# Latent attention: probabilities as the stationary operand, the result divided with queries on partitions and turned by TensorE

## The chip, the cores and the metric

The kernel runs on one core of one Trainium2 chip. A core has TensorE (matmuls), VectorE, ScalarE, GpSimd and SyncE, which run side by side and wait for each other through semaphores; DMA engines move data between the chip's memory (HBM) and the on-chip SBUF. TensorE writes into PSUM. In the profile the engines are called PE (TensorE's matmuls), PEld (its weight loads, that is loads of the stationary operand), DVE (VectorE), ACT (ScalarE), POOL (GpSimd) and SP (SyncE). The metric is the device time of one execution in microseconds. The kernel before takes 2379.64 us (median of 3 runs, 2379.31 to 2381.75).

## The reference

Two layers on 1024 tokens of width 1024, in float32. Layer 0 mixes tokens by differential attention, layer 1 by latent attention; each is followed by a gated MLP with a causal convolution, and a norm closes the whole. The change is in the latent attention of layer 1 alone. Cut to that:

```python
def mla_attention(h, w_in, q_norm_g, kv_norm_g, w_uq, w_ukv, w_o, cos, sin):
    ...                                   # q_nope, q_pe, k_nope, k_pe, v from latents; 16 heads
    scale = (MLA_NOPE + MLA_ROPE) ** -0.5         # (64 + 32) ** -0.5
    def block(args):                              # one block of 128 queries
        qn, qp, blk = args
        sc = (jnp.einsum('bqhd,bkhd->bhqk', qn, k_nope)
              + jnp.einsum('bqhr,bkr->bhqk', qp, k_pe)).astype(jnp.float32) * scale
        p = masked_softmax(sc, chunk_mask(blk, s)[None, None])
        return jnp.einsum('bhqk,bkhe->bqhe', p.astype(v.dtype), v)   # v has 64 columns per head
    ...
    return o.reshape(b, s, MLA_HEADS * MLA_V) @ w_o
```

The mask lets a query see the keys of its own chunk of 64 tokens and of all chunks before it. So query block i (128 queries) needs i + 1 key blocks of 128.

## The kernel before

Numbers are split into a high and a low part of a reduced float format (fp32r); a product of two split numbers takes three matmuls (`mm3`, lines 119 to 121), each with a stationary and a moving operand. `hi` (line 127, a cast, mostly on ACT) makes the high part and `lo` (line 130, a subtraction on DVE or POOL) the low one.

The latent attention works in 64 steps, 16 heads of 4 (`MlaStep`, line 1981; `attend`, line 1781). Step p of a head treats query blocks 2p and 2p + 1, so 256 queries. The order of p is 1, 0, 3, 2, and 3, 2, 1, 0 in the last head. A step does:

- `scores(j)` for its two query blocks j: queries stationary, keys moving, 3 matmuls per 512 keys, into PSUM "S" (two buffers of 1024 columns); a memset for the mask (line 1999), the row maximum (line 2000), then exp with the sum l of each row (line 2001). Queries are on partitions.
- `weigh(j)` (line 2005): a reciprocal of l on DVE (line 2007) and a multiplication of all probabilities of the block by it on POOL (`scale`, line 149).
- `turn` (line 254): 128x128 blocks of probabilities are transposed by TensorE (line 263, four or three into one bank of PSUM "b") and split by `hi` and `lo` into `pt[g]`, keys on partitions. A full group holds in this order: first key block for query block 0, the same for query block 1, second key block for 0, for 1. The last group leaves out what the mask hides and holds three blocks.
- `product` (line 2010): for each key block of 128, V is stationary (128 keys on partitions; 64 columns of its high part and 64 of its low part side by side) and the transposed probabilities are moving, low part and then high part, 256 queries wide, or 128 for the last key block. The result in PSUM "u" (one buffer) has V's columns on partitions: 64 for the high part of V, 64 for the low. ACT copies one half and DVE adds the other (lines 2024, 2025) into a tile `o` of 64x512 for each head and half of the tokens, and when its two steps are done a DMA on ACT's queue writes it to `o_d` in HBM (line 2027). `finish` does nothing.

`steps` (line 292) writes the work of neighbouring steps interleaved: step t's scores and the key and query projections of the next pair of heads (`units`, `q_unit`, `k_unit`), step t - 1's transposes between the two scores, and its product after the second; `finish` is called for step t - 2. The projections of the last pair are done before its steps start, so its steps have none beside them. Within a layer's attention here no order is written out by hand (there is one for the other attention, `manual_schedule`); the order of instructions on each engine is chosen when the program is built, by a planner that runs its own simulation with its own costs (`schedule_with_timeline_sim`, line 2314), from the dependences and the written order. On the chip each engine then works in that fixed order.

Beside the attention POOL and DVE split weights and values of the next pair (`split_w`, `split_v`), and, in the last 10 steps, the output projection's weights are fetched and split. The output projection reads `o_d` back, 128 tokens at a time and four pairs of heads at once (`project_load`, line 659), with the columns of two heads on 128 partitions.

Of the kernel before, what the change touches and what calls it, by code (L numbers as in the profile page):

```python
# [17 lines left out]

P = 128
S = 1024  # L20
D = 1024
NT = S // P
KD = D // P
EPS = 1e-6
# [12 lines left out]
FFN = 2816  # L37
NF = FFN // P


def blocks(n, step=512):
    return [(a, min(step, n - a)) for a in range(0, n, step)]


class Ring:


    def __init__(self, k, *places):
        self.k, self.places, self.n = k, places, 0
# [7 lines left out]
class Trunk:  # L57
# [7 lines left out]
    def __init__(self, tc, ctx, a):  # L65
# [226 lines left out]
    def steps(self, attend, units, prepare, n, apart=False):  # L292


        steps = []
        for t in range(n + 2):
            now = before = None
            u = []
            if t < n:
                now = attend(t)  # L300
                steps.append(now)
                prepare(t)
                u = units(t)
                now.scores(0)
            if 0 < t <= n:
                before = steps[t - 1]
            alone = u[:-1] if apart else []
            if alone:
                u = u[-1:]
            self.run(alone or u, 2 if alone else 1)  # L310
            if before:
                before.turn()
            self.run(alone)
            if now:
                now.weigh(0)
                now.scores(1)
            self.run(u)
            if before:
                before.product()
            if now:  # L320
                now.weigh(1)
            if t >= 2:
                steps[t - 2].finish()
            yield
# [1331 lines left out]
    def mla_heads(self, cT, v_d, o_d):  # L1656
        nc, a = self.nc, self.a
        pairs = MLA_HEADS // 2
        heads = [dict() for _ in range(MLA_HEADS)]
# [4 lines left out]
        cs = self.at("u13", [P, S])  # L1664
        nc.sync.dma_start(cs, a["rope_q"])
        R = SimpleNamespace(
            P=self.ring("u12", "u6", "u7", "u8", "u9"), pT=self.ring("u0", "u1", "u10", "u11"), o=self.ring("h4", "h5", "h6", "h7"),
        )

        eng = lambda x: {"S": None, "V": nc.vector, "P": nc.gpsimd}[x]  # L1670
# [129 lines left out]
class Step:  # L1800


    def __init__(self, k, R, h, p, heads):
        self.k, self.R, self.h, self.p, self.hd, self.heads = k, R, h, p, heads[h], heads
        self.l, self.probs = [], []

    def turn(self):
        self.pt = self.k.turn(self.R.pT, self.p, self.probs)
# [2 lines left out]
class DaStep(Step):  # L1811
# [37 lines left out]
    def scores(self, j):  # L1849
        k, nc, hd = self.k, self.k.nc, self.hd  # L1850
        i = 2 * self.p + j
        n = (i + 1) * P
        q = hd["q"][i // 4]
        qs = slice((i % 4) * P, (i % 4 + 1) * P)
        sc = self.sc[j] = []
        for c in range(2):
            if c == 0 or not self.one:
                ps = k.big()
            sc.append(ps[:, c * 512 : c * 512 + n] if self.one else ps[:, :n])
        self.both[j] = ps.rearrange("p (c n) -> p c n", c=2)  # L1860
# [65 lines left out]
    def product(self, g):  # L1926
        k, p = self.k, self.p
        if self.o is None:
            self.o = k.bank()[:, :256]
        for kb, (ah, al), c0 in k.key_blocks(p, {x: self.pt.get(x, self.pt[g]) for x in range(p + 1)}):  # L1930
            if kb // 2 == g:
                vh, vl = (self.hd["v"][kb // 4][:, part, (kb % 4) * P : (kb % 4 + 1) * P] for part in range(2))
                k.mm3(self.o[:, c0:], vh, vl, ah, al, kb == 0, kb == 2 * p + 1)
# [47 lines left out]
class MlaStep(Step):  # L1981
    def __init__(self, k, R, h, p, heads, V, o_d):
        super().__init__(k, R, h, p, heads)
        self.V = V
        self.dst = o_d[h // 2, (h % 2) * 64 : (h % 2) * 64 + 64, (p // 2) * 512 : (p // 2 + 1) * 512]

    def scores(self, j):
        k, nc = self.k, self.k.nc
        i = 2 * self.p + j
        n = (i + 1) * P  # L1990
        q, kt = self.hd["q"], self.hd["k"]
        qs = slice(i * P, (i + 1) * P)
        nm, l = k.stat(), k.stat()
        if j == 0 or n > 512:
            self.e = self.R.P([P, S])
        sc, e = k.big()[:, :n], self.e[:, :n] if n > 512 else self.e[:, j * 512 : j * 512 + n]
        for b, m in blocks(n):
            k.mm3(sc[:, b : b + m], q[:, 0, qs], q[:, 1, qs], kt[:, 0, b : b + m], kt[:, 1, b : b + m], True, True)
        nc.vector.memset(sc[0:64, n - 64 : n], NEG)
        nc.vector.tensor_reduce(nm, sc, axis=AX.X, op=ALU.max, negate=True)  # L2000
        nc.scalar.activation(e, sc, AF.Exp, bias=nm, accum_out=l)
        self.l.append(l)
        self.probs.append(e)

    def weigh(self, j):
        nc, l, e = self.k.nc, self.l[j], self.probs[j]
        nc.vector.reciprocal(l, l)  # L2007
        self.k.scale(e, l[:, 0:1], "P")

    def product(self):  # L2010
        k, nc, h, p = self.k, self.k.nc, self.h, self.p
        cols = slice((p % 2) * 256, (p % 2 + 1) * 256)
        half = p // 2
        first = ("o", half) not in self.hd
        if first:
            self.hd["o", half] = self.R.o([64, 512])
        t = self.hd["o", half]
        o = k.bank("u")[:, :256]
        for kb, (ah, al), c0 in k.key_blocks(p, self.pt):
            v = self.V[h // 2][:, kb, h % 2].rearrange("p a e -> p (a e)")  # L2020
            nc.tensor.matmul(o[:, c0:], v, al, start=kb == 0, stop=False)  # L2021
            nc.tensor.matmul(o[:, c0:], v, ah, start=False, stop=kb == 2 * p + 1)  # L2022

        nc.scalar.copy(t[:, cols], o[64:128])
        nc.vector.tensor_add(t[:, cols], t[:, cols], o[0:64])
        if not first:
            nc.scalar.dma_start(self.dst, t)

    def finish(self):
        pass  # L2030


def kernel_body(tc, a, out):
    with ExitStack() as ctx:
# [144 lines left out]
        heads = k.mla_input(W_in, hts, turns, v_d, lambda cT: k.mla_heads(cT, v_d, o_d[1]))  # L2179
        W = []  # L2180
        step, finish, rest = prefetcher(a["mla_w_o"], W, slots(2, 3, 6, 7, 1, 10, 0, 11), units(6, 7, 8, 9))
        heads.rest(step)
        finish()
        places = iter(units(2, 3, 4, 5, 12, 13, 10, 11))
        X = k.project_first(W, o_d[1], k.ring(*halves(0, 1, 2, 3)), x_d[1], lambda q, i: k.at(next(places), [P, D]), 0, rest)
# [132 lines left out]
```

## Time and profile before

The profiled execution took 2379.93 us, of which the span from the first to the last instruction is 2378.1 us.

| | |
|---|---|
| median of 3 runs | 2379.64 us |
| profiled execution, its span | 2379.93 us, 2378.1 us |
| mean granted TensorE clock | 0.999 |
| busy: PE, PEld, DVE, ACT, POOL | 2346.4, 1975.7, 1925.3, 1246.5, 587.5 us |
| first and last product of the latent attention | 1312 us and 1650 us after the span's start |
| matmuls of the product (lines 2021 and 2022) | 640, of them 512 with 256 columns and 128 with 128 |
| transposes of the probabilities (line 263) | 576 |
| reciprocals (line 2007), copies and additions of the result (lines 2024, 2025) | 128, 64 and 64 |
| DMA writes of the result (line 2027) | 32 of 128 KB |

How to read it: "busy" is the union of an engine's records, and TensorE's records are as long as a matmul takes from entering to leaving the array, so that neighbours overlap; what a matmul costs a busy TensorE is the distance to the start of the next. A group's row gives line, engine, operation, what is written and read, the shapes, the count, then busy time, mean length in ns, and the idle time of the engine before it with what ended it. A row of waits gives who waited for whom, the total in us, how often, and, where there is a third number, the longest.

### The profile page before, as it was taken

The page shows a single profiled execution, that of the slowest core. Times are in us where ns is not written, and L with a number is a line of the kernel's source. Part 1 is how long each engine was busy: PE and PEld are TensorE (multiplying, and loading weights), DVE is VectorE, ACT ScalarE, POOL GpSimd, SP SyncE. Part 2 cuts the span into 40 slices and gives each one's busy share as a digit, 9 for nine tenths or more (in the row PEclk, how much of TensorE's full clock was granted, in tenths as well). Part 3 has the DMA queues.
Part 4 walks back from the last instruction along what each step waited for, and adds up shares of the span by engine and source line. Part 5 has one row for each costly group of instructions (what it writes and reads, how often), then busy time and mean ns, then how long its engine had stood idle before and what let it go on. Part 6 is the DMA issues. An engine that isn't in the chain of part 4 may idle for free.

```text
span 2378.1 us, 32958 instructions
## 1 busy us (share of the span) xinstructions
PE 2346.4 (99%) x12146; PEld 1975.7 (83%) x12146; DVE 1925.3 (81%) x3170; ACT 1246.5 (52%) x2301; POOL 587.5 (25%) x465
## 2 busy tenths in 40 slices
PE   9999999999999999999999999999999999999998
PEld 7888888788888888888898889988788888888886
DVE  6777877859888888999855888886588888889997
ACT  5666666745444444354444778775354444443544
POOL 4545444324000000000133666673420000000001
PEclk9999999999999999999999999999999999999999
DMA  3111111342222222652221211133322222227502
GB/s 148 40 36 36 49 37 54 114 130 86 93 84 80 80 88 81 233 176 84 84 98 56 72 33 39 41 98 114 108 72 94 82 80 80 89 80 283 177 1 80
DMA packets 95667, 213.42 MB, mean 90 GB/s; under 512 B 8713, under 2 KB 33937, under 8 KB 95505
## 3 DMA queue, kind: packets, MB, share of 16 engines
q1 hardware_dynamic: 86304, 183.51, 23.6%
q10 hardware_dynamic: 9200, 27.80, 3.2%
q8 instruction: 96, 1.57, 0.3%
q14 instruction: 67, 0.54, 0.1%
HBM read 158.85 MB, written 52.43 MB: 89 GB/s over the span
## 4 chain that ended last, share of the span: by engine, by line
PE 89%; DVE 5%; DMA 2%; ACT 2%; issue 1%; POOL 0%; POOLq 0%; DVEq 0%; ACTq 0%; SPq 0%
PE S L119 13%; PE S L121 13%; PE S L120 13%; PE b L119 9%; PE b L120 8%; PE b L121 8%; PE u L119 5%; PE u L121 4%; PE u L120 4%; PE S L1866 3%; PE b L263 2%; PE u L2022 1%; PE u L2021 1%; PE b L1912 1%; DVE s L130 1%
## 5 line engine op out<-in xcount | busy, mean ns | idle before, releaser
L167 POOL TENSOR_TENSOR st<-st,mhalf 128x1 f32<-128x1 f32 x56 | 35.4, 633 | 1301.5 <-DVE st L164 1291.4
L121 PE MATMUL S<-s,u 128*128 128x512 f32 (+1 forms) x800 | 301.3, 377 | 1.1 <-POOL u L130 1.0
L119 PE MATMUL S<-s,u 128*128 128x512 f32 (+1 forms) x800 | 301.8, 377 | 0.2 <-ACT u L1092 0.2
L120 PE MATMUL S<-s,u 128*128 128x512 f32 (+1 forms) x800 | 301.0, 376 | 0.0
L127 ACT CAST u<-h 128x512 fp32r<-128x512 f32 (+1 forms) x194 | 115.8, 619 | 274.4 <-DVE h L1013 262.2
L119 PE MATMUL b<-s,u 128*128 128x512 f32 x588 | 230.8, 393 | 1.1 <-DVE u L130 0.4
L120 PE MATMUL b<-s,u 128*128 128x512 f32 x588 | 229.0, 389 | 0.0
L121 PE MATMUL b<-s,u 128*128 128x512 f32 x588 | 229.0, 389 | 0.0
L1070 DVE SCALAR_TENSOR_TENSOR u<-u,conv,u 128x1023 f32<-128x1023 f32 (+1 forms) x176 | 225.0, 1278 | 0.8 <-ACT u L1066 0.7
L149 POOL TENSOR_TENSOR u<-u,st 128x512 f32<-128x512 f32 (+7 forms) x160 | 173.2, 1091 | 161.4 <-DVE st L2007 107.5
L127 ACT CAST s<-u 128x512 fp32r<-128x512 f32 (+3 forms) x229 | 144.0, 663 | 97.8 <-PE u L121 28.3
L127 ACT CAST u<-b 128x512 fp32r<-128x512 f32 (+1 forms) x256 | 134.8, 547 | 92.1 <-PE b L1912 57.7
L130 DVE TENSOR_TENSOR u<-b,u 128x512 fp32r<-128x512 f32 (+1 forms) x256 | 158.5, 631 | 23.7 <-ACT u L127 22.6
L121 PEld LDWEIGHTS S<-s,u 128*128 128x128 f32 x800 | 150.5, 188 | 29.2 <-POOL u L130 1.4
L119 PEld LDWEIGHTS S<-s,u 128*128 128x128 f32 x800 | 150.5, 188 | 27.9 <-ACT u L1092 0.5
L120 PEld LDWEIGHTS S<-s,u 128*128 128x128 f32 x800 | 150.6, 188 | 27.2
L119 PE MATMUL u<-s,s 128*128 128x512 f32 (+1 forms) x408 | 165.2, 405 | 1.1 <-DVE s L130 0.9
L121 PE MATMUL u<-s,s 128*128 128x512 f32 (+1 forms) x408 | 158.3, 388 | 0.0
L120 PE MATMUL u<-s,s 128*128 128x512 f32 (+1 forms) x408 | 157.6, 386 | 0.0
L130 DVE TENSOR_TENSOR s<-u,s 128x512 fp32r<-128x512 f32 (+2 forms) x205 | 140.7, 720 | 16.4 <-ACT s L127 15.9
L1073 ACT ACTIVATE u<-u 128x1024 f32<-128x1024 f32 x44 | 46.7, 1062 | 187.6 <-DVE u L1070 187.6
L130 DVE TENSOR_TENSOR u<-h,u 128x512 fp32r<-128x512 f32 x171 | 117.9, 689 | 32.4 <-ACT u L127 31.5
(290 smaller groups left out, 6384.9 us busy)
## 6 DMA issues: line engine op xcount, KB each, us to landing
u<-in_ffn_up SPq DMA_DIRECT2D x88, 512.0 KB, 4.2
g_d<-u ACTq DMA_DIRECT2D x44, 512.0 KB, 2.6
u<-in_ffn_down SPq DMA_DIRECT2D x66, 256.0 KB, 4.9
u<-g_d SPq DMA_DIRECT2D x62, 256.0 KB, 3.9
s<-in_da_wqkv SPq DMA_DIRECT2D x23, 512.0 KB, 3.3
x_d<-u SPq DMA_DIRECT2D x16, 512.0 KB, 3.0
s<-x_d SPq DMA_DIRECT2D x8, 1024.0 KB, 10.8
s<-g_d SPq DMA_DIRECT2D x18, 256.0 KB, 5.3
```

The source lines that it names most:

```text
L119: mm(out, lh, rl, start=first, stop=False, skip_group_check=onto)
L120: mm(out, lh, rh, start=False, stop=False, skip_group_check=onto)
L121: mm(out, ll, rh, start=False, stop=last, skip_group_check=onto)
L127: self.nc.scalar.copy(out, src)
L130: (eng or self.nc.vector).tensor_sub(out, src, hi.bitcast(F32))
L149: self.nc.gpsimd.tensor_mul(x, x, s.to_broadcast(list(x.shape)))
L167: nc.gpsimd.tensor_tensor(r, s, self.mhalf, ALU.pow)
L263: self.nc.tensor.transpose(ps[:, j * P : (j + 1) * P], probs[t][:, k : k + P], self.ident)
L1070: nc.vector.scalar_tensor_tensor(t[half][:, back:], u[half][:, : S - back], w, t[half][:, back:], ALU.mult, ALU.add)
L1073: nc.scalar.activation(t[0], t[0], AF.Silu)
L1866: nc.tensor.matmul(sc[c][:, b : b + m], q[rows, qp, qs], kt[rows, kp, :m], start=x == 0, stop=x == 2)
L1912: k.nc.tensor.transpose(ps[:, j * P : (j + 1) * P], self.e[t][0][:, c : c + P], k.ident)
```

## The change

The product's operands change places. For each of the two query blocks and each key block that it may see, the transposed probabilities (128 keys x 128 queries; low part, then high part) are stationary and V (128 keys x 128 columns, high and low part side by side) is moving. The result has queries on partitions, in PSUM "u": for each query block 64 columns for the high and 64 for the low part of V.

The probabilities are no longer scaled: `weigh` goes. Both row sums of a step stand in one tile of two columns, one reciprocal inverts both, and after ACT's copy of the low half and DVE's addition of the high half, POOL multiplies the 128x128 result by the inverse row sums. The results of the two heads of a pair stand side by side in one tile of 128 queries x 4 query blocks x 128 columns for each half of the tokens. `finish` of every step with odd head and even p turns this tile: four transposes by TensorE into one bank of "b", a copy by ACT, and one DMA of 128x512 to `o_d` from ACT's queue. The layout of `o_d` stays.

```diff
@@ steps @@
             self.run(alone)
             if now:
-                now.weigh(0)
                 now.scores(1)
             self.run(u)
             if before:
                 before.product()
-            if now:
-                now.weigh(1)
             if t >= 2:
                 steps[t - 2].finish()
...
@@ mla_heads @@
-            P=self.ring("u12", "u6", "u7", "u8", "u9"), pT=self.ring("u0", "u1", "u10", "u11"), o=self.ring("h4", "h5", "h6", "h7"),
+            P=self.ring("u12", "u6", "u7", "u8", "u9"), pT=self.ring("u0", "u1", "u10", "u11"), o=self.ring("h4", "h5", "h6", "h7"), oT=self.ring("h12", "h13"),
...
@@ MlaStep @@
-        self.dst = o_d[h // 2, (h % 2) * 64 : (h % 2) * 64 + 64, (p // 2) * 512 : (p // 2 + 1) * 512]
+        self.dst = o_d[h // 2, :, (p // 2) * 512 : (p // 2 + 1) * 512]
+        self.pair = heads[h - h % 2]
+        self.l = k.stat(2)
...
-    def weigh(self, j):
-        nc, l, e = self.k.nc, self.l[j], self.probs[j]
-        nc.vector.reciprocal(l, l)
-        self.k.scale(e, l[:, 0:1], "P")
 
     def product(self):
...
-        for kb, (ah, al), c0 in k.key_blocks(p, self.pt):
-            v = self.V[h // 2][:, kb, h % 2].rearrange("p a e -> p (a e)")
-            nc.tensor.matmul(o[:, c0:], v, al, start=kb == 0, stop=False)
-            nc.tensor.matmul(o[:, c0:], v, ah, start=False, stop=kb == 2 * p + 1)
-
-        nc.scalar.copy(t[:, cols], o[64:128])
-        nc.vector.tensor_add(t[:, cols], t[:, cols], o[0:64])
-        if not first:
+        for x in range(2):
+            for kb in range(2 * p + x + 1):
+                v = self.V[h // 2][:, kb, h % 2].rearrange("p a e -> p (a e)")
+                c = (kb % 2 * 2 + x if kb // 2 < p else kb % 2 + x) * P
+                for part in (1, 0):
+                    nc.tensor.matmul(o[:, x * P : x * P + P], self.pt[kb // 2][part][:, c : c + P], v,
+                                     start=kb == 0 and part == 1, stop=kb == 2 * p + x and part == 0)
+        y = o.rearrange("p (x a e) -> p x a e", x=2, a=2)
+        nc.vector.reciprocal(self.l, self.l)
+        nc.scalar.copy(out, y[:, :, 1])
+        nc.vector.tensor_add(out, out, y[:, :, 0])
+        nc.gpsimd.tensor_mul(out, out, self.l.unsqueeze(2).to_broadcast([P, 2, 64]))
+
+    def finish(self):
+        k, nc = self.k, self.k.nc
+        if self.h % 2 and self.p % 2 == 0:
+            ps = k.bank()
+            for j in range(4):
+                nc.tensor.transpose(ps[:, j * P : (j + 1) * P], self.o[:, j], k.ident)
+            t = self.R.oT([P, 512])
+            nc.scalar.copy(t, ps)
             nc.scalar.dma_start(self.dst, t)
```

More of the change, by code (lines that the diff above doesn't have):

```diff
@@ L1804, in __init__ @@
         self.k, self.R, self.h, self.p, self.hd, self.heads = k, R, h, p, heads[h], heads
-        self.l, self.probs = [], []
+        self.probs = []
     def turn(self):
@@ L1992, in scores @@
         qs = slice(i * P, (i + 1) * P)
-        nm, l = k.stat(), k.stat()
+        nm, l = k.stat(), self.l[:, j : j + 1]
         if j == 0 or n > 512:
@@ L2001, in scores @@
         nc.scalar.activation(e, sc, AF.Exp, bias=nm, accum_out=l)
-        self.l.append(l)
         self.probs.append(e)
-    def weigh(self, j):
-        nc, l, e = self.k.nc, self.l[j], self.probs[j]
-        nc.vector.reciprocal(l, l)
-        self.k.scale(e, l[:, 0:1], "P")
     def product(self):
         k, nc, h, p = self.k, self.k.nc, self.h, self.p
-        cols = slice((p % 2) * 256, (p % 2 + 1) * 256)
         half = p // 2
[L2014 to L2017, printed above, removed]
+        if ("o", half) not in self.pair:
+            self.pair["o", half] = self.R.o([P, 4, P])
@@ L2018, in product @@
+        self.o = self.pair["o", half]
+        out = self.o[:, 2 * (p % 2) : 2 * (p % 2) + 2, (h % 2) * 64 : (h % 2) * 64 + 64]
         o = k.bank("u")[:, :256]
-        for kb, (ah, al), c0 in k.key_blocks(p, self.pt):
-            v = self.V[h // 2][:, kb, h % 2].rearrange("p a e -> p (a e)")
-            nc.tensor.matmul(o[:, c0:], v, al, start=kb == 0, stop=False)
-            nc.tensor.matmul(o[:, c0:], v, ah, start=False, stop=kb == 2 * p + 1)
-        nc.scalar.copy(t[:, cols], o[64:128])
@@ L2027, in product @@
             nc.scalar.dma_start(self.dst, t)
-    def finish(self):
-        pass
 def kernel_body(tc, a, out):
```

## The prediction

> **What bounds the kernel now.** First the page: who is busy, at what clock, and which chain ends last.
>
> ```profile
> span 2378.1 us, 32958 instructions
> ...
> PE 2346.4 (99%) x12146; PEld 1975.7 (83%) x12146; DVE 1925.3 (81%) x3170; ACT 1246.5 (52%) x2301; POOL 587.5 (25%) x465
> ...
> PEclk9999999999999999999999999999999999999999
> ...
> PE 89%; DVE 5%; DMA 2%; ACT 2%; issue 1%; POOL 0%; POOLq 0%; DVEq 0%; ACTq 0%; SPq 0%
> ```
>
> TensorE is 99% busy and is 89% of the chain that ended last, at full clock. That is a mean over stages, so the second view is the stage that the change touches, cut into stretches. Columns: stretch and its length, then busy time and instructions of PE (matmuls), PEld (weight loads), DVE, ACT, POOL, then the granted clock, DMA share and GB/s.
>
> ```profile
> 1310.00:1370.00 60.00, 57.94 (x356) 50.20 (x355) 50.90 (x119) 47.01 (x99) 40.01 (x30) 1.00 0.23 70
> ...
> 1411.52:1453.04 41.52, 41.52 (x273) 37.56 (x272) 34.37 (x86) 32.15 (x70) 27.80 (x22) 1.00 0.14 39
> 1453.04:1494.56 41.52, 41.52 (x273) 37.56 (x272) 34.37 (x86) 32.15 (x70) 27.82 (x22) 1.00 0.13 39
> ...
> 1560.00:1630.00 70.00, 67.39 (x455) 60.44 (x454) 58.88 (x141) 54.55 (x118) 46.85 (x37) 1.00 0.27 78
> ...
> 1310.00:1652.00 342.00, 337.32 (x2176) 301.59 (x2175) 278.85 (x664) 257.50 (x555) 216.74 (x171) 1.00 0.22 65
> ```
>
> Two heads take 41.52 us, twice with the same 273 matmuls and with PE busy for all of it; the next engine, DVE, has 7 us to spare. In the whole stage PE idles 342.00 - 337.32 = 4.68 us: 2.06 at the start, 2.61 where the last pair has no projections left to fill gaps. So a matmul added here lengthens the stage by its own time, and what is taken from POOL, DVE or ACT gives back at most those 4.7 us.
>
> **What a matmul costs in this stream.** A record's length (0.28 us) is not its price, since the records overlap; the price is the distance between starts. The third view is the order in time of PE around two products (start us, length us, what):
>
> ```profile
> 1451.25 0.31 PE L119 MATMUL S<-s,s 128*128 128x128 f32 x1
> 1451.39 0.27 PE L120 MATMUL S<-s,s 128*128 128x128 f32 x1
> 1451.50 0.28 PE L121 MATMUL S<-s,s 128*128 128x128 f32 x1
> 1451.62 0.45 PE L119 MATMUL b<-s,u 128*128 128x512 f32 x1
> ...
> 1452.36 0.39 PE L119 MATMUL b<-s,u 128*128 128x512 f32 x1
> 1452.59 0.39 PE L120 MATMUL b<-s,u 128*128 128x512 f32 x1
> ...
> 1454.52 0.28 PE L2021 MATMUL u<-u,s 128*128 128x256 f32 x1
> ...
> 1456.07 0.28 PE L2022 MATMUL u<-u,s 128*128 128x256 f32 x1
> 1456.19 0.22 PE L2021 MATMUL u<-u,s 128*128 128x128 f32 x1
> 1456.25 0.28 PE L2022 MATMUL u<-u,s 128*128 128x128 f32 x1
> 1456.36 0.95 PE L263 MATMUL b<-ident,u 128*128 128x128 f32 x7
> 1457.07 0.48 PE L119 MATMUL S<-s,s 128*128 128x512 f32 x1
> ```
>
> From 1454.52 to 1456.07 stand 14 matmuls of 256 columns in a row (seven key blocks, low and high part): 1.55 / 13 = 0.119 us each; 512 columns take 0.23. By these two, 128 columns would stream in some 0.06, and one does (1456.19 to 1456.25). But the next needs 0.11, and so do the 128-column score matmuls (1451.39 to 1451.50 to 1451.62). The weight loads say why:
>
> ```profile
> 1451.22 0.19 PEld L119 LDWEIGHTS S<-s,s 128*128 128x128 f32 x1
> 1451.33 0.19 PEld L120 LDWEIGHTS S<-s,s 128*128 128x128 f32 x1
> 1451.45 0.19 PEld L121 LDWEIGHTS S<-s,s 128*128 128x128 f32 x1
> 1451.56 0.19 PEld L119 LDWEIGHTS b<-s,u 128*128 128x128 f32 x1
> ```
>
> Each matmul has a load of its own, and the loads follow each other at (1451.56 - 1451.22) / 3 = 0.113 us. A matmul of 256 columns just covers that; one of 128 does not, except a first one whose successor was loaded ahead.
>
> **The change, part by part.** *The product* (lines 2021 and 2022). Its present instructions, by form (columns: count | busy us, mean ns):
>
> ```profile
> L2021 PE MATMUL u<-u,s 128*128 128x256 f32 x256 | 68.0, 294 | 0.2 <-DVE h L2025 0.2
> L2022 PE MATMUL u<-u,s 128*128 128x256 f32 x256 | 65.1, 282 | 0.0
> L2022 PE MATMUL u<-u,s 128*128 128x128 f32 x64 | 17.7, 277 | 0.0
> L2021 PE MATMUL u<-u,s 128*128 128x128 f32 x64 | 14.3, 223 | 0.0
> ```
>
> 512 of 256 columns and 64 pairs of 128. A pair costs 1456.19 to 1456.36 = 0.17. Sum before: 512 x 0.119 + 64 x 0.17 = 60.9 + 10.9 = 71.8 us.
>
> After, a step p has 2(4p + 3) matmuls, all of 128 columns and each with its own stationary block of probabilities: 6 + 14 + 22 + 30 = 72 per head, 1152 in 16 heads. The streamed columns stay the same (512 x 256 + 128 x 128 = 1152 x 128); the weight loads go from 640 to 1152. At 0.113 that is 130.2; as in the pair above I let the first matmul of each of the 64 products have 0.06, less 64 x 0.053 = 3.4: 126.8 us. **Plus 55.0.** The ends of this price: below, 0.061, if every load were hidden (70.3 us, so -1.5); next, 0.101, the mean of the seven transposes (1456.36 to 1457.07; 116.4 us, +44.6); above, 0.123, the three score matmuls counted from the first start (0.37 / 3; 141.7 us, +69.9). I take 0.113, since it is the steady distance of the same operand type and both 128-column runs show it.
>
> *The turning back* (finish): four transposes for each of 8 pairs x 2 halves, 64 in all, at the 0.101 of the row x7: **plus 6.5**; 7.2 if they take 0.113.
>
> *What leaves and comes on the other engines*, all from the stage:
>
> ```profile
> 1310.00:1652.00 342.00, 143.13 (x125) 1.00 0.22 65
> ...
> L149 POOL TENSOR_TENSOR u<-u,st 128x128 f32<-128x128 f32 x15 | 6.0, 403 | 1.6 <-DVE st L2007 0.9
> ...
> L2024 ACT COPY h<-u 64x256 f32<-64x256 f32 x64 | 23.7, 370 | 11.8 <-PE u L2022 10.7
> ...
> L127 ACT CAST u<-b 128x512 fp32r<-128x512 f32 x96 | 54.6, 588 | 4.6 <-PE b L263 2.0 <-PE u L2022 0.7
> ...
> L2025 DVE TENSOR_TENSOR h<-h,u 64x256 f32<-64x256 f32 x64 | 26.1, 408 | 15.7 <-ACT h L2024 14.7
> ...
> L2007 DVE RECIPROCAL st<-st 128x1 f32<-128x1 f32 x124 | 18.8, 151 | 7.9 <-ACT u L2001 7.6
> ```
>
> The first row is line 149 alone, POOL's scaling of the probabilities: 143.1 us leave POOL, and 64 multiplications of 128x128 come, 64 x 0.403 = 25.8. DVE loses 64 of its 128 reciprocals (64 x 0.151 = 9.7) and adds 128 columns instead of 256 (at most the present 0.408 each). ACT copies 128 columns instead of 256 (at most 0.370), and gains 16 copies of 512 columns (16 x 0.588 = 9.4); its issues of the result's DMA fall from 32 to 16. None of it is on the path while PE is busy throughout: PE's own work hides it. On the latency of one step, the transposes no longer wait for a reciprocal and a multiplication by POOL after exp, at least 0.151 + 0.403 = 0.55 us and more for wider rows; that matters only where PE idles. Of the 4.7 us of idling I take back a little under half, since the rest of that chain (reduction, exp, cast, subtraction) stays: **minus 2** (ends: 0 and -4.7).
>
> *Waits that come.* The product writes the one bank "u", which must be emptied before the next product. Today this is all that it costs (the first two rows; the third is the split of a weight on POOL):
>
> ```profile
> PEld u L2021 <- DVE h L2025: 0.5, 1, 0.5
> ...
> PE u L2021 <- DVE h L2025: 0.2, 1, 0.2
> ...
> L130 POOL TENSOR_TENSOR s<-h,s 128x512 fp32r<-128x512 f32 x27 | 34.8, 1290 | 1.0 <-ACT s L127 0.4
> ```
>
> Steps are 41.52 / 8 = 5.2 us apart, and emptying takes 0.37 + 0.41 after the last matmul, so this stays. The transposes of a finish follow the product one step later in the written order, so POOL's 0.4 us and what is queued ahead of it (a split of 1.3 us) should be over: nothing, with the price if not below. Behind a transpose that waited stand the next scores and, after them, every cast and exp.
>
> *The sum*: 55.0 + 6.5 - 2 = +59.5 on the profiled execution's own 2379.93 (span 2378.1 and 1.8 around it): 2439.4. The runs' median, 2379.64, lies 0.3 lower: **2439 us**, 2.5% slower. The stage's regular part should go from 41.52 to 41.52 + 2 x (72 x 0.113 - 4 x 0.053 - 4.49) + 8 x 0.101 = some 49.2 us per pair (4.49 = 71.8 / 16).
>
> **The rivals.** *Weight loads half hidden* (between 0.06 and 0.11, say their mean, 0.087): for it, that loads are pulled ahead of a running matmul in the pair at 1456.19; against it, that the second one never is, and that the score matmuls pay 0.11 twice running. 1152 x 0.087 = 100.2, +28.4 + 6.5 - 2: 2412 us. The Trainium skill (TensorE: Matmul & The Clock Gate, section "Back-to-back issue gap") gives such a pace: a sustained stream of load and matmul pairs at about 81 ns for 128 columns, and 131 ns for 512. By 81 the estimate would be 1152 x 0.081 - 71.8 + 6.5 - 2 = +26. The rows here show 0.23 where it has 131 ns, so its 81 has little weight.
>
> *Weight loads fully hidden*, which is the case on the other side: 1152 x 0.061 = 70.3, so -1.5 + 6.5 - 2 = +3: 2383, no difference that can be measured, and 2380 with all of the idling back. It decides from a steady distance of 0.065 us or less. For it, the columns streamed are unchanged and one row shows 0.06; against it, the 0.113 between loads, and that 0.06 is seen only for a matmul that follows a longer one.
>
> *A new wait on PE*: the transposes reach PE before POOL's multiplication is over, because POOL stands in a split. 16 finishes x 1.3 us = 21 more: 2460. For it, POOL still has such splits; against it, the step between, and 117 us less on POOL.
>
> **How the numbers follow.** Forecast 0.80, half hidden 0.08, fully hidden 0.05, new wait 0.07. The likeliest gives 2439. The low end takes the 0.101 price with all idling back, 44.6 + 6.5 - 4.7 = +46.4, and a little of the half-hidden case: 2424. The high end takes 0.123 with nothing back, 69.9 + 7.2 = +77, or 2457, of which I leave out the last part, as both 128-column runs show 0.113 after their first: 2452. About 0.2% (5 us) is what a measurement of this kernel can tell from no change. Only the fully hidden case falls inside that, and with everything on its side just beyond: faster 0.01, same 0.04, slower 0.95.
>
> **What would show it.** Right: the distance of starts in the longest product (30 matmuls) is 0.11 us throughout, PE stays at 100% in the regular stretches, a pair takes 49 us, POOL falls by some 117 us without the end moving for it, and before and after the stage nothing changes by more than a us or two. Wrong: distances of 0.06 to 0.09 (the price of a load), PE idle before the transposes with POOL as releaser (the new wait), or gaps before L119 and L263 that were busy before (another order from the planner). If a pair came back at 42 us, the whole account of the weight loads would be wrong.

## The result, and the profile after

The changed kernel takes 2456.51 us (median of 6 runs, 2453.36 to 2458.47) against 2379.89 us before (6 runs): a ratio of 1.0321, 95% interval 1.031 to 1.0332. The forecast was 2439, in a range up to 2452: the sign was right, 17 us are missing. The profiled execution is the fastest of the six, 2453.36 us, so the profile explains 73.4 us of span (2451.5 against 2378.1).

The page of the changed kernel:

```profile
span 2451.5 us, 33680 instructions
...
PE 2411.7 (98%) x12722; PEld 2037.9 (83%) x12722; DVE 1912.9 (78%) x3106; ACT 1243.4 (51%) x2317; POOL 469.8 (19%) x401
...
PE 89%; DVE 6%; issue 2%; ACT 2%; DMA 1%; POOL 1%; POOLq 0%; DVEq 0%; SPq 0%; ACTq 0%
```

POOL lost 117.7 us as expected, and TensorE carries 65 us more. But it is busy for 98% instead of 99%. Where, is read from the stage. The stage of the kernel before, from its first scores (1292 us) to its last product:

```profile
1290.00:1651.00 361.00, 354.93 (x2262) 315.82 (x2261) 294.36 (x699) 269.09 (x587) 228.69 (x181) 1.00 0.22 65
```

and of the changed one, with two stretches of the length of a pair of heads and three of 5 us:

```profile
1290.00:1725.00 435.00, 420.53 (x2837) 378.47 (x2835) 282.65 (x635) 264.55 (x601) 110.33 (x116) 0.99 0.17 53
...
1403.90:1455.74 51.84, 50.48 (x350) 45.69 (x349) 33.59 (x78) 31.05 (x73) 12.93 (x14) 1.00 0.10 31
1455.74:1507.74 52.00, 49.95 (x346) 45.13 (x344) 32.95 (x77) 31.47 (x73) 12.92 (x14) 1.00 0.10 31
...
1520.00:1525.00 5.00, 4.05 (x25) 3.29 (x24) 3.03 (x10) 2.73 (x6) 3.13 (x3) 0.87 0.09 12
1525.00:1530.00 5.00, 5.00 (x29) 4.45 (x27) 2.51 (x7) 2.97 (x8) 0.00 (x0) 0.79 0.38 145
...
1635.00:1640.00 5.00, 4.00 (x13) 3.14 (x14) 4.06 (x10) 3.96 (x12) 0.40 (x1) 0.66 0.38 105
```

A pair takes 52 us, not 49.2, and PE idles in both pairs shown, for 1.36 and 2.05 us. In the whole stage it idles 435.00 - 420.53 = 14.5 us, against 361.00 - 354.93 = 6.1 before. DVE has more room than before (65% busy in the stage, against 82%), so no other engine became the bound in its sum of work. And the clock, which stood at 1.00 all through the stage before, falls at two places (0.87 and 0.79, then 0.66).

The distances between starts, summed over the stage up to the last product, split the 73.4 us:

| TensorE, by what the distance follows | before | after | difference | forecast |
|---|---|---|---|---|
| product (640 and 1152 matmuls) | 77.0 | 132.0 | +54.9 | +55.0 |
| turning back (60 of 64 lie in it) | - | 6.5 | +6.5 | +6.5 |
| everything else | 283.1 | 296.4 | +13.3 | -2 |
| after the stage | 727.9 | 726.5 | -1.4 | 0 |

So both prices were right, and the miss is the third row: idle time (8.4 us more) and the lower clock, (0.13 + 0.21 + 0.34) x 5 = 3.4 us by estimate. That is 11.8 of the 13.3 us; the other 1.5 were not located. The order in time of PE shows both the price and one of the gaps:

```profile
1462.40 1.09 PE L2016 MATMUL u<-s,u 128*128 128x128 f32 x8
...
1466.26 1.68 PE L2016 MATMUL u<-s,u 128*128 128x128 f32 x14
1467.77 0.51 PE L263 MATMUL b<-ident,u 128*128 128x128 f32 x3
1468.03 0.42 PE L119 MATMUL S<-s,s 128*128 128x384 f32 x1
1468.29 0.33 PE L120 MATMUL S<-s,s 128*128 128x384 f32 x1
1468.46 0.34 PE L121 MATMUL S<-s,s 128*128 128x384 f32 x1
1469.75 1.90 PE L2016 MATMUL u<-s,u 128*128 128x128 f32 x14 [0.95 <-DVE h L2021]
```

14 matmuls from 1466.26 to 1467.77 are 0.108 us each; over all 1152 the median distance is 0.112. These 14 and the 8 from 1462.40 on are one product (p = 2), which ends at 1466.26 + 1.68 = 1467.94. The product of the next step (p = 1, the second x14) starts 1.8 us after that end, and for 0.95 us of this PE stands until DVE's addition (line 2021) has emptied bank u. What DVE did meanwhile:

```profile
1466.53 0.67 DVE L130 TENSOR_TENSOR s<-b,s 64x512 fp32r<-64x512 f32 x1
1467.12 0.94 DVE L1999 TENSOR_REDUCE st<-S 128x1 f32<-128x768 f32 x1
1467.98 0.67 DVE L130 TENSOR_TENSOR u<-b,u 128x512 fp32r<-128x512 f32 x1
1468.68 0.69 DVE L130 TENSOR_TENSOR s<-b,s 64x512 fp32r<-64x512 f32 x1
1469.41 0.29 DVE L2021 TENSOR_TENSOR h<-h,u 128x128 f32<-128x128 f32 x1
```

and ACT:

```profile
1467.97 0.27 ACT L2020 COPY h<-u 128x128 f32<-128x128 f32 x1 [0.16 <-PE u L2016]
1468.13 1.05 ACT L127 CAST s<-u 128x1024 fp32r<-128x1024 f32 x1
1469.08 0.48 ACT L127 CAST u<-b 128x384 fp32r<-128x384 f32 x1
1469.45 0.92 ACT L2000 ACTIVATE u<-S,st 128x768 f32<-128x768 f32 x1
```

ACT copies as soon as the product is over; the addition comes 1.17 us after the copy's end (1468.24), because two subtractions stand before it in DVE's fixed order. Elsewhere it is the other way round, and DVE stands waiting for the copy. Over all 64 products of each trace, the addition ends 1.77 us after the product's last matmul in the mean before the change and 1.11 us after it: the emptying has not become slower. But the next product now starts within 2 us of that last matmul's end in 17 of 63 cases, against 3 before. The waits of the stage, PE's first, then ACT's and DVE's (total us, times, longest):

```profile
PE S L119 <- ACT u L2000: 7.5, 12, 1.7
PE u L2016 <- DVE h L2021: 5.2, 7, 1.0
...
ACT u L2000 <- DVE st L1999: 57.2, 52, 2.7
DVE h L2021 <- ACT h L2020: 38.8, 31, 2.4
```

PE waits 7.5 us for exp (line 2000) to release a bank of scores and 5.2 for the emptying of bank u. Before, the second was 0.2, and the first, in the stage of the kernel before:

```profile
PE S L119 <- ACT u L2001: 2.2, 3, 1.4
```

(PEld has rows for the same waits. The expectations below add both, "13.3" and "18"; on PE alone it is 5.2 and 7.5.) What is behind them was tested.

### The profile page after: what moved, and what is told of

Its sections match the earlier page's. It is cut to its first block, busy times and chain, and to the rows that moved or that the text cites. A ratio compares the mean times of both kernels' runs of the same rounds, so it can differ in the third digit from the quotient of the medians.

```text
span 2451.5 us, 33680 instructions
## 1 busy us (share of the span) xinstructions
PE 2411.7 (98%) x12722; PEld 2037.9 (83%) x12722; DVE 1912.9 (78%) x3106; ACT 1243.4 (51%) x2317; POOL 469.8 (19%) x401
## 4 chain that ended last, share of the span: by engine, by line
PE 89%; DVE 6%; issue 2%; ACT 2%; DMA 1%; POOL 1%; POOLq 0%; DVEq 0%; SPq 0%; ACTq 0%
PE S L119 13%; PE S L121 13%; PE S L120 13%; PE b L119 8%; PE b L120 8%; PE b L121 8%; PE u L119 5%; PE u L121 4%; PE u L120 4%; PE u L2016 4%; PE S L1863 3%; PE b L263 2%; PE b L1909 1%; DVE s L130 1%; DVE u L130 1%
## 5 line engine op out<-in xcount | busy, mean ns | idle before, releaser
L119 PE MATMUL S<-s,u 128*128 128x512 f32 (+1 forms) x800 | 301.8, 377 | 0.2 <-ACT u L1089 0.2
L119 PE MATMUL b<-s,u 128*128 128x512 f32 x588 | 232.4, 395 | 0.2 <-DVE u L130 0.2
L119 PEld LDWEIGHTS S<-s,u 128*128 128x128 f32 x800 | 150.5, 188 | 28.0 <-ACT u L1089 0.5
L119 PE MATMUL u<-s,s 128*128 128x512 f32 (+1 forms) x408 | 165.1, 405 | 1.1 <-DVE s L130 0.9
L2016 PE MATMUL u<-s,u 128*128 128x128 f32 x1152 | 147.6, 274 | 5.5 <-DVE h L2021 5.2
L2016 PEld LDWEIGHTS u<-s,u 128*128 128x128 f32 x1152 | 141.3, 191 | 10.9 <-DVE h L2021 8.1
```

What stands on the lines that cost most here:

```text
L119: mm(out, lh, rl, start=first, stop=False, skip_group_check=onto)
L2016: nc.tensor.matmul(o[:, x * P : x * P + P], self.pt[kb // 2][part][:, c : c + P], v, start=kb == 0 and part == 1, stop=kb == 2 * p + x and ...
```

## The experiments

Differences (with a plus sign) are to the median of the kernel before, measured anew beside each version: 2378.7 to 2379.2.

**The price of the weight loads.** Without the change of operands, the same number of matmuls:

```diff
-            nc.tensor.matmul(o[:, c0:], v, al, start=kb == 0, stop=False)
-            nc.tensor.matmul(o[:, c0:], v, ah, start=False, stop=kb == 2 * p + 1)
+            for c in range(c0, 256, P):          # each block of 128 queries by itself
+                nc.tensor.matmul(o[:, c : c + P], v, al[:, c - c0 : c - c0 + P], ...)
+                nc.tensor.matmul(o[:, c : c + P], v, ah[:, c - c0 : c - c0 + P], ...)
```

> The kernel before (V stationary, scaling by POOL, no turning back) with each moving block of 256 queries cut into two matmuls of 128: 1152 matmuls and weight loads instead of 640, as in the changed kernel, and nothing else. If the price is the pace of the weight loads (0.113 us each), 55 us more than before: 2435, from 2430 to 2440, with PE full throughout. If a fresh block of probabilities as the stationary operand is what costs, and loads of V are hidden, 2380 to 2385. If 128-column matmuls also upset the order of the engines, 2440 to 2450 with PE idle in the stage.

Measured 2443.94 (ratio 1.0271, 1.0254 to 1.0288): +64.8. Its PE in order of time, with V stationary throughout:

```profile
1456.62 0.22 PE L2023 MATMUL u<-u,s 128*128 128x128 f32 x1
1456.68 0.28 PE L2024 MATMUL u<-u,s 128*128 128x128 f32 x1
...
1457.35 0.28 PE L2024 MATMUL u<-u,s 128*128 128x128 f32 x1
```

0.06 once, then 0.67 / 6 = 0.112: the same pace with the other operand stationary, so it is the pace of 128-column matmuls with a load each, not of fresh probabilities. The product's distances sum to 129.4 us, 52.3 more than before. More than half of the other 12 us is idle time here too. Its stage shows

```profile
1290.00:1714.00 424.00, 410.96 (x2781) 367.64 (x2781) 301.30 (x700) 272.73 (x588) 230.01 (x181) 1.00 0.18 56
```

13.0 us of it, 6.9 more than before, and PE's longest waits are again for exp at the scores (6.3 us). (Of the rest, some 1.7 us are a fall of the clock at 503 us, ahead of the stage.) Two runs added PE work of another shape, the first matmul of 256 columns repeated:

```diff
+            for _ in range((2, 5, 9, 13)[p] if kb == 0 else 0):       # second run: (0, 1, 2, 3)[p]
+                nc.tensor.matmul(o[:, c0:], v, al, start=True, stop=True)
             nc.tensor.matmul(o[:, c0:], v, al, start=kb == 0, stop=False)
```

> The kernel before with its own first matmul of each product (256 columns, started anew each time, so that the result is the same) repeated 2, 5, 9 or 13 times for p = 0 to 3: 464 more matmuls of 0.119 us, 55 us of PE, the same amount that the split to 128 columns brought, but with 256 columns. If any PE work added there brings idle time with it (a longer product, so later emptying and exp), 2441 to 2447 as in the split version. If the idle time of that version comes from its many short matmuls and their order, 2433 to 2437.

> The kernel before with 96 of the repeated matmuls of 256 columns instead of 464 (0, 1, 2, 3 for p = 0 to 3), 11.4 us of PE. If idle time grows with the PE work added (10 us for 55), 2391 to 2394. If any added work makes the planner lay out another, worse order, the 10 us come at once: 2398 to 2404.

Measured 2445.18 (+66.0) with 464 more matmuls and 2390.08 (+11.3, interval of the ratio 1.0032 to 1.0061) with 96. The small dose costs its 11.4 us and no idle time (6.0 us in the stage, 6.1 before); the large one brings some 11 us on top of its 55, as the split did. So short matmuls are not needed for such a loss. But it is idle time only in part: in the profiled execution, the slowest of the four (2449.32), PE idles 4.5 us more than before, and the clock stands at half for 17 us in all, which by half of that time is worth some 8.5 us. The fastest, at a mean clock of 0.999 instead of 0.995, took 2439.85. The order on the engines changed as well, so two doses do not show that the loss grows with the work.

**The single bank u.** First, halves of the bank by turns, then one of the three banks b:

```diff
-        o = k.bank("u")[:, :256]
+        ...                                                    # u: one tile of bank u and a count, for each pair
+        o = u[0][:, u[1] % 2 * 256 : u[1] % 2 * 256 + 256]     # its halves by turns
```

```diff
-        o = k.bank("u")[:, :256]
+        o = k.bank()[:, :256]
```

> The changed kernel with the product's results in the two halves of bank u by turns, so that a product need not wait for the emptying of the one before. If the waits of the product for DVE's addition (13 us in the changed profile) are the unforeseen loss, 2442 to 2448. If they only come where the order already is late, 2453 to 2457, with the same idle time in front of other instructions.

> The changed kernel with the product's result in one of the three banks b instead of the single bank u, so that the wait of a product for the emptying of the one before is really gone (the version with two halves of bank u still showed the same waits, 13.3 us). If these waits are the loss, 2442 to 2447. If they are a place where a late order shows, PE waits elsewhere and the time is 2452 to 2457; more than that if the transposes and projections miss the bank.

Measured 2454.55 and 2507.58. The first tests nothing: by the traces, the order of instructions on PE, DVE, ACT and POOL is that of the changed kernel throughout the stage, and PE's wait for the addition is still 5.2 us. It is the changed kernel measured once more, 2 us lower. In the second, three kinds of work share three banks, and PE waits for them in many places:

```profile
PE b L2016 <- DVE u L130: 16.7, 19, 1.4
PE S L119 <- ACT u L2000: 15.1, 23, 1.3
PE b L263 <- DVE u L130: 14.5, 20, 1.1
```

Then the loops, key blocks outside:

```diff
-        for x in range(2):
-            for kb in range(2 * p + x + 1):
+        for kb in range(2 * p + 2):
+            for x in range(kb // (2 * p + 1), 2):
```

> The changed kernel with the loops of the product exchanged, key blocks outside and query blocks inside, so that both query blocks advance with each group of transposed probabilities, as in the kernel before. Same instructions, same counts. If the loss comes from the second query block's matmuls all standing behind the last group, 2440 to 2446. If the single bank or the order of exp and scores is the cause whatever the loop order, 2453 to 2458.

Measured 2450.09 (1.0281 to 1.0312), 6.4 less than the changed kernel's 2456.51, in runs from 2445.52 to 2453.16. That is between the two ranges named. PE's wait at bank u fell from 5.2 to 0.2 us, but the one at the scores stayed at 6.1, against 7.5; PE idles 10.7 us in the stage. The product's waits are a part, not the whole. In the profiled execution (2450.98) the clock also fell twice, which cost some 6.8 us (an estimate: half of the time at half clock); the fastest run had a mean clock of 0.999.

**The missing scaling.** In the kernel before, without reciprocals and scaling; then with POOL's work kept but out of the chain; then with transposes written later in the step:

```diff
     def weigh(self, j):
-        nc.vector.reciprocal(l, l)
-        self.k.scale(e, l[:, 0:1], "P")
+        pass
```

```diff
-        self.k.scale(e, l[:, 0:1], "P")
+        ...                                  # for each 512 columns, m of them from c on
+            nc.gpsimd.tensor_mul(junk[:, :m], e[:, c : c + m], l[:, 0:1].to_broadcast([P, m]))
```

```diff
-            if before:
-                before.turn()
             self.run(alone)
             if now:
                 now.weigh(0)
                 now.scores(1)
+            if before:
+                before.turn()
```

> The kernel before without reciprocals and scaling (the division of the softmax is left out altogether). It shows what 143 us less on POOL and a shorter step are worth where PE is full. By the prediction 2 us less, 2375 to 2380. If a shorter step let PE run without its idle time, 2372 to 2375. If the missing scaling changes the planner's order for the worse, over 2382, and then a part of the changed kernel's loss has that cause.

> The kernel before with the reciprocals and POOL's multiplications kept, but written into unused tiles, so that the transposes follow exp directly (the division is left out, as in the version without scaling). If the 20 us of that version come from the transposes' standing right behind exp, 2393 to 2401. If they come from POOL's being idle, 2378 to 2384.

> The kernel before without scaling (the division is left out), with the transposes written after the second scores as in the run above. If the 20 us that the missing scaling cost come from transposes laid right behind exp, 2376 to 2384. If they come from anything else (less work on POOL, the clock), 2395 to 2400.

Measured 2398.83, 2392.87 and 2388.04 (1.0024 to 1.0053). Taking 143 us away from POOL makes the kernel before 19.7 us **slower**. In the first of these, PE waits in front of the transposes, now directly behind exp:

```profile
PE b L263 <- ACT u L2001: 9.4, 9, 1.7
PE b L263 <- DVE u L130: 2.7, 6, 1.0
```

There is no such row for exp before, when POOL's scaling stood between. With POOL's work kept but off the chain 13.7 of the 19.7 us remain, so most of it is not POOL's idleness. But there PE waits only 1.9 us for exp in front of the transposes, of 13.7 us of idle time in the stage; its largest wait is for the subtraction of `lo` there, 4.4 us. Written later, the transposes give 10.8 us back, again between the two ranges named. In all three the order on every engine is another one. So it is shown that taking the scaling out of the chain costs time here, and only argued that the cause is the lost distance between exp and the transposes. Then the changed kernel with its scaling as before:

```diff
+                now.weigh(0)
                 now.scores(1)
...
+                now.weigh(1)
...
-        nc.gpsimd.tensor_mul(out, out, self.l.unsqueeze(2).to_broadcast([P, 2, 64]))
```

> The changed kernel with the scaling of the probabilities kept as before (reciprocal and POOL's multiplication between exp and the transposes) and without POOL's multiplication of the result: the operands change places, the result is turned, and nothing else. If the missing scaling costs by itself what it cost in the kernel before (20 us, the run without scaling), this gives much of it back: 2440 to 2446. If it cost that only there, and the swap brings its own loss, 2451 to 2458.

Measured 2446.94 (1.027 to 1.0301): 9.6 us less than the changed kernel, although POOL does 120 us more. So a part of the loss does go with the division's new place, or with the order that comes with it.

**The written order, and repairs put together.** The late transposes in both kernels, the second scores last, and combinations with the exchanged loops:

```diff
             self.run(u)
             if before:
                 before.product()
+            if now:
+                now.scores(1)
```

> The changed kernel with one step's transposes written after the second scores of the next step instead of between the two: the planner gives scores and projections the first right to PE, and the transposes more time after exp. If the loss is an order that puts PE's instructions right behind an exp that comes late, 2440 to 2447. If it is the length of the product or the bank, 2453 to 2458.

> The kernel before with nothing changed but the place of the transposes in the written order (after the second scores). Without scaling that place gave 11 us back. If it does so because the transposes then stand clear of exp, the kernel before, whose transposes already wait for POOL's scaling, gains nothing or loses a little: 2377 to 2386. If it is a better order in itself, 2368 to 2376.

> The changed kernel with the second scores of a step written last, behind the transposes and the product of the step before. PE waits 18 us in the changed kernel's stage for a bank of scores that exp has not yet released; written later, the scores ask for it later. If PE's waits come from scores laid just behind the exp that frees their bank, 2440 to 2448. If a wait taken away there only moves, as with the exchanged loops, 2450 to 2458.

> The run above with the product's loops exchanged too, which took the product's own waits (13.3 us) down to 1: both kinds of wait at once. If they are independent, 2437 to 2443, the predicted sum. If one order only trades waits for others, 2447 to 2457.

> The changed kernel with both repairs: the scaling of the probabilities kept on POOL (none of the result), and the product's loops exchanged. If both losses add up, 2437 to 2442, which is the predicted sum of weight loads and transposes alone. If they are one loss in two guises, 2444 to 2449.

Measured 2455.52, 2379.81 (no difference to before: 0.9992 to 1.0012), 2455.59, 2448.32 and 2457.02. The first four say nothing about the written order: by the traces, the planner laid out the same order as without the edit. On PE, DVE, ACT and POOL, the instructions of the stage follow each other in the first and third as in the changed kernel, in the second as in the kernel before, in the fourth as in the version with exchanged loops alone. So 2455.52 and 2455.59 are the changed kernel once more, and 2448.32 is the exchanged loops once more (2450.09). They show how far such medians differ: some 2 us.

The last one does have another order. That the exchanged loops take back all that the kept scaling gained, and end above both ranges named, is mostly the clock. PE's idle time in the stage is 12.6 us, against 10.4 with the kept scaling alone, but three times the clock stood at half for 6.8 us, which cost some 10 us by the same estimate. Three stretches of it:

```profile
1505.00:1510.00 5.00, 5.00 (x26) 5.00 (x26) 0.34 (x2) 0.52 (x3) 0.87 (x2) 0.50 0.00 0
...
1560.00:1565.00 5.00, 5.00 (x22) 4.74 (x22) 0.29 (x1) 0.85 (x2) 0.22 (x1) 0.50 0.00 0
...
1615.00:1620.00 5.00, 5.00 (x19) 4.31 (x19) 0.29 (x1) 0.85 (x2) 0.00 (x0) 0.50 0.14 52
```

The kept scaling alone has no such stretch in its stage. The four runs of the two together have mean clocks of 0.993 to 0.996, those of the kept scaling alone 0.998 and 0.999.

**The hand-over at bank u.** The result now has the high and low half on the same partitions, so one instruction can empty the bank; or ACT alone, with POOL adding:

```diff
-        nc.scalar.copy(out, y[:, :, 1])
-        nc.vector.tensor_add(out, out, y[:, :, 0])
+        nc.vector.tensor_reduce(out, o.rearrange("p (x a e) -> p x e a", x=2, a=2), axis=AX.X, op=ALU.add)
```

```diff
-        nc.scalar.copy(out, y[:, :, 1])
-        nc.vector.tensor_add(out, out, y[:, :, 0])
+        z = self.R.z([P, 4, 64])
+        nc.scalar.copy(z, o.rearrange("p (a e) -> p a e", e=64))
+        z = z.rearrange("p (x a) e -> p x a e", a=2)
+        nc.gpsimd.tensor_add(out, z[:, :, 1], z[:, :, 0])
```

> The changed kernel with bank u emptied by one instruction on DVE (a sum over the high and the low half, which now lie on the same partitions) instead of ACT's copy and DVE's addition. DVE waited 39 us for that copy, and the product 13 us for the addition. If the hand-over from ACT to DVE is what makes the order late, 2443 to 2450. If not, 2453 to 2458.

> The changed kernel with bank u emptied by ACT alone (a copy of all 256 columns) and the addition of the high and low halves made by POOL from SBUF: the other way to have one engine instead of two at the bank, with nothing of it on DVE. If the hand-over, in which DVE stands waiting for ACT's copy and all its later reductions with it, is the unforeseen loss, this comes out near the version emptied by DVE alone: 2438 to 2446. If that version won because ACT was relieved of the copy, 2450 to 2458.

Measured 2441.10 (1.0241 to 1.0275) and 2439.25 (1.0246 to 1.028): 15.4 and 17.3 us less than the changed kernel (14.3 and 16.1 by the differences to the kernel before beside each), and 2.1 and 0.3 us above the forecast of 2439. The stage with DVE alone, and PE's waits in it:

```profile
1290.00:1715.00 425.00, 419.70 (x2865) 380.58 (x2865) 295.52 (x638) 253.72 (x541) 111.39 (x117) 1.00 0.17 55
```

```profile
PE u L2016 <- DVE h L2020: 1.8, 4, 0.7
PE S L119 <- ACT u L2000: 1.7, 4, 0.8
```

and with ACT alone:

```profile
1290.00:1712.00 422.00, 416.57 (x2837) 377.56 (x2836) 267.96 (x568) 268.11 (x597) 140.78 (x179) 1.00 0.17 55
```

```profile
PE S L119 <- ACT u L2000: 1.3, 3, 0.9
PE u L2016 <- ACT h L2021: 0.8, 5, 0.2
```

PE idles 5.3 and 5.4 us instead of 14.5, less than in the kernel before, and both kinds of wait shrink together, also the one for exp at the scores, which the edits do not touch. From the product's last matmul to the end of the emptying of bank u, 0.72 and 0.68 us pass in the mean, instead of 1.11. Since emptying by either engine works, the load of one of them is not the reason; the hand-over between the two is the likely one. Not excluded is that another order alone did it, since both edits also brought another order on every engine. The exchanged loops on top:

> The version emptied by DVE alone with the product's loops exchanged too. The time left above the predicted sum is 2 us, so if that is idle time at the product's bank, 2437 to 2440; if the exchange costs idle time elsewhere, as it did beside the kept scaling, 2443 to 2452. In neither case is it faster than the kernel before.

Measured 2445.34, 4 us more than without them, and only 4.8 less than with the exchanged loops alone: beside those, the single emptying is worth a third. No version with the operands exchanged came near the kernel before: 60 us of weight loads and transposes remain.

## Why the prediction was right and wrong

**Right: the bound and the two prices.** TensorE set the time of the stage; the product's distances rose by 54.9 us where 55.0 stood, with a median of 0.112 us where 0.113 was read from four weight loads; the transposes cost what they were given. (Both sums of the product are 5 us above the forecast's, 77.0 for 71.8 and 132.0 for 126.8, in different places: before, 3.0 us of it lie at the first matmul of each uninterrupted run of the product's matmuls and 1.9 at the last; after, 3.8 at the last. That the difference agrees to 0.1 us is in part luck.) The two rivals with hidden loads fell: the steady distance is 0.112 us with either operand stationary, and 0.06 stands only at a group's first matmul. The 81 ns that the Trainium skill gives for a sustained stream of 128 columns (TensorE: Matmul & The Clock Gate, section "Back-to-back issue gap") differ from that; the measurement decides. After the stage nothing moved by more than 1.4 us.

**Wrong: "minus 2" for the idle time, and "nothing" for the waits that come.** Together they stood for -2 and measured +13.3. Two steps of the reasoning failed.

The first was that bank u "stays" because steps are 5.2 us apart and emptying takes 0.37 + 0.41. Both sides of that comparison were wrong. The mean step is not the distance that counts: it is the time from the end of one product to the start of the next, which was within 2 us 3 times before and 17 times after. And emptying is not the sum of two durations: it is two places in two engines' fixed orders, and took 1.77 us in the mean already before. In the gap shown, the copy came at once and the addition 1.17 us after it. PE's own wait at bank u is 5.2 us in the stage. The two runs that put the emptying on one engine got 14 to 17 us back, nearly the whole miss; in them the wait for exp at the scores shrank too. Which part of that is the hand-over and which the new order is open.

The second was that a shorter chain can only help: "what is taken from POOL, DVE or ACT gives back at most those 4.7 us". The kernel before without scaling loses 19.7 us, and the changed kernel with the scaling kept gains 9.6. So by these runs the term "minus 2" has the wrong sign: the order is laid out ahead, and with a step taken out of the chain it came out worse. The prediction had left the planner out as a cause and named it only as a sign ("gaps before L119 and L263 that were busy before"), and the gaps before L119 are what was seen (7.5 us, against 2.2).

A third term was not in the sum at all: the clock fell twice in the stage, some 3.4 us.

The rival with a new wait on PE came out near the measured time (2460) by luck: transposes waiting for POOL took 0.2 us in the stage.

**What stays open.** Why the split version and the one with repeated matmuls lose some 11 us more than their added PE work of 52 to 55 us (6.9 and 4.5 of it idle time in the profiled stage), and the one with 11 us of work does not, was not separated: they keep the hand-over of the kernel before, but emptying by one engine was not tried there, where the two halves lie on different partitions. Nor was it shown which part of the gain from the single emptying is the wait removed and which is another order by the planner, as each edit that had an effect changed the order of all engines. Whether another written order would help the changed kernel was not tested, since none of those tried reached the engines. The kept scaling and the single emptying were not run together.

## What to carry to other kernels

When TensorE is full, count distances between starts, and for every edit count the weight loads: a 128-column matmul that needs its own load costs nearly as much as one of 256 columns (0.112 against 0.119 us here), so exchanging operands is free only if the moving side stays wide. A bank that two engines empty one after the other depends on two fixed orders; if a change brings its writers closer, try to let one engine empty it (14 to 17 us here, but 5 beside the exchanged loops). Do not cost a removed step at zero because nothing waited for it: where the order is planned ahead, removing it can bring a worse order (19.7 us here), and the way to know is to run the old kernel without it. And before a result is read as the effect of an edit, compare the order of instructions in the two traces: five edits here left it as it was.

## What was not expected of the hardware

The granted clock falls inside the stage, and the gaps ahead of it are short. In the changed kernel PE stood 0.95 us before 1521.76, its only gap of more than 0.06 us in the nine us ahead of the fall, and the clock was 0.87 and 0.79 in two stretches of 5 us there: it stood at 0.50 for 3.4 us from 1523.67 on, and again from 1636.31 on, after a gap of 1.68 us. Its 512-column matmuls then stood 0.43 us apart instead of 0.23:

```profile
1523.86 0.63 PE L120 MATMUL S<-s,s 128*128 128x512 f32 x1
1524.29 0.63 PE L121 MATMUL S<-s,s 128*128 128x512 f32 x1
```

The Trainium skill (TensorE: Matmul & The Clock Gate, section "HAM oscillation — how this bites in real kernels") gives gaps above some 3.4 us as what to avoid; here the clock fell after gaps of 0.95 and 1.68 us, so that figure is no safe bound. But such a gap is not enough by itself. The same 0.95 us at 1469.75 had no such consequence, and the kernel before, with gaps of up to 1.39 us in its stage, had no fall there. What decides was not tested.

Wherever the clock fell before the last 10 us of a program, it stood at half for 3.4 or 6.8 us, and the executions of one kernel differ in it. With the exchanged loops the clock fell twice in the profiled execution, 6.8 us lost by the estimate above, and the four runs took 2445.52, 2449.20, 2450.98 and 2453.16 us at mean clocks of 0.999, 0.997, 0.996 and 0.996. So gaps can cost more than their length here, and make the time less steady; and a difference of a few us between two versions is only read rightly beside their clocks.
